# Segment sums of a Mamba-2 (SSD) branch: one fp32 matmul with fp32 operands, or two float32r matmuls over the high and low part of dt*A

## The chip, the cores and the metric

The kernel runs on one core of a Trainium2 chip. The time is device microseconds of one execution of the whole program, as the median of several runs. The profile is one execution taken by the hardware profiler. The engines of the core run their own instruction streams in order and wait for each other through semaphores: TensorE (PE, matmuls; PEld is its weight load), VectorE (DVE), ScalarE (ACT), GpSimd (POOL) and SyncE (SP, here only the queue of the weight transfers).

## The reference

The program is a two-layer decoder trunk on 256 tokens of width 1024. Layer 0 is SwiGLU, a mixer "AB", SwiGLU and a gated embedding; layer 1 has another mixer. The change lies in mixer AB, which runs two branches on the same input and joins them in one output projection:

```python
def ssd_chunked(x, dt, a, bmat, cmat):            # 16 heads, 4 groups, chunks of 128 tokens
    a_cum = cumsum(dt * a)                        # per head, within a chunk
    seg = a_cum[:, :, :, None] - a_cum[:, :, None, :]
    decay = exp(where(causal, seg, -inf))
    scores = einsum('bclgn,bcsgn->bclsg', cc, bc)
    y_diag = einsum(..., scores[..., None] * decay, xdt)
    ...                                           # plus the state carried from chunk 0 to chunk 1
def s5_mixer(u, ...):                             # second branch
    ...                                           # complex linear recurrence, giving y
    y = gelu(y)
    return y * sigmoid(y @ w_glu + b_glu)
def mixer_ab(x, ...):
    return concatenate([ssd_mixer(...), s5_mixer(...)], -1) @ w_out
```

## The kernel before, in words

Every large fp32 product is made of three float32r matmuls: each operand is split into a high part (rounded by ScalarE: names with `h`, as `wh`, `yh`, `xh`) and the rest (by VectorE: `wl`, `yl`, `xl`). Weights arrive in units of 1 MB (`wst`) and are split when they arrive.

The order of the instructions on each engine is set when the program is built: a scheduler places them, within the data dependencies and the buffers that a tile's tag has (`bufs=2`: the third tile of a tag waits until the first has been read). A tag's buffers go round in the order in which the code asks for tiles.

Mixer AB (`mixer_ab`) has, in the part that matters here:

- **S5 branch.** Eight batches give `s5y`; ScalarE copies each into `G`. When the second half of `G` is complete, ScalarE applies Gelu to it, GpSimd's queue writes it to DRAM (`ydram`) and reads it back transposed (`yT`), ScalarE and VectorE split it (`yh`, `yl`), and TensorE uses it in the 192 matmuls of `s5_outputs` (`glu`: eight channel tiles of 24). Half of the 24 need only the first half of `G`. After each channel tile come `th` (tanh, ScalarE), `gt` (VectorE), and its split `s5h`, `s5l`.
- **SSD branch.** For each of four groups `ssd_decays` makes a score tile `sc` (masked: `scm`) and for each of two chunks the product `R` = lower-triangular mask times dt*A (VectorE, 128x512), the segment sums `seg` = `strict` x `R` (TensorE), `E` = exp(seg) (ScalarE) and `E`*`scm` (VectorE). `ssd_heads` multiplies (`yp`, `cp`), adds and gates (`y`), takes the squares (`sq`, ScalarE) for a norm and scales; `finish_heads` transposes (`yT_ssd`) and splits (`xh_ssd`, `xl_ssd`). The decays of group 0 are emitted earlier, in `ab_inputs` (`first`).
- **Join.** `out_project` (`acc_ab`) multiplies the S5 parts and then the SSD parts with the output weights.

PSUM tiles `sc`, `seg`, `cp`, `ea_ps` and the S5 tiles share the tag `mm` with two buffers; `yp` and `yT_ssd` share `tr` with two. `sq` has two buffers of its own, and so has `gt`.

Gelu and Exp are in different function tables of ScalarE; a change of table is an instruction of its own (ACT_TABLE_LOAD).

Of the kernel before, what the change touches and what calls it, by code (L numbers as in the profile page):

```python
# [17 lines left out]
P = 128  # L18
D = 1024
NTOK = 256  # L20
NT = 2
# [12 lines left out]
def f32(ap):  # L34
    return ap.bitcast(F32)
# [298 lines left out]
def bc(ap, axis, n):  # L334

    shape = list(ap.shape)
    shape.insert(axis, n)
    return ap.unsqueeze(axis).broadcast_to(shape)
# [390 lines left out]
def s5_outputs(g, pool, yT, yh, yl):  # L729

    nc = g.nc
    hb = pool.tile([P, KT], F32, tag="hb", name="hb", bufs=1)
    nc.scalar.mul(hb, g.cols("bglu"), 0.5)
    sh = pool.tile([P, KT, NTOK], F32R, tag="sh", name="s5h", bufs=1)
    sl = pool.tile([P, KT, NTOK], F32R, tag="sl", name="s5l", bufs=1)
    for u in range(4):
        pieces = g.w.unit()
        for j in range(2):
            ct = 2 * u + j
            wh, wl = (p.rearrange("p (k c) -> p k c", k=KT) for p in pieces[j])  # L740
            ps = g.ps.tile([P, NTOK], F32, tag="acc", name=f"glu_{ct}", bufs=4)
            for k in range(KT):
                nc.tensor.matmul(ps, wh[:, k, :], yh[:, k, :], start=k == 0, stop=False)
                nc.tensor.matmul(ps, wh[:, k, :], yl[:, k, :], start=False, stop=False)
                nc.tensor.matmul(ps, wl[:, k, :], yh[:, k, :], start=False, stop=k == KT - 1)
            th = pool.tile([P, NTOK], F32, tag="th", name=f"th_{ct}", bufs=2)
            nc.scalar.activation(th, ps, AF.Tanh, scale=0.5, bias=hb[:, ct:ct + 1])
            gt = pool.tile([P, NTOK], F32, tag="gt", name=f"gt_{ct}", bufs=2)
            by_token = lambda ap: ap.rearrange("p (s c) -> p c s", s=4)
            nc.vector.scalar_tensor_tensor(gt.rearrange("p (c s) -> p c s", s=4), by_token(th[:, :]), 1.0,  # L750
                                           by_token(yT[ct // 4][:, ct % 4, :]), op0=ALU.add, op1=ALU.mult)
            nc.scalar.mul(sh[:, ct, :], gt, 0.5)
            nc.vector.scalar_tensor_tensor(sl[:, ct, :], gt, 0.5, f32(sh[:, ct, :]), op0=ALU.mult, op1=ALU.subtract)
    return sh, sl


def ssd_steps(g, pool, raw):

    nc = g.nc
    ps = g.ps.tile([P, NT, 16], F32, tag="mm", name="dt_ps", bufs=2)  # L760
    for t in range(NT):
        nc.tensor.matmul(ps[:, t, :], raw[:, t * P:(t + 1) * P], g.cst("fold")[0:32, :], start=True, stop=True)
    row = pool.tile([P, 48], F32, tag="abrow", name="abrow", bufs=1)
    nc.scalar.dma_start(row, g.abrow.broadcast_to([P, 48]))
    v = pool.tile([P, NT, 16], F32, tag="dtv", name="dtv", bufs=1)
    nc.vector.tensor_tensor(v, ps, bc(row[:, 0:16], 1, NT), op=ALU.add)
    e = softplus_terms(g, v, [P, NT, 16], pool, "dt")
    nc.vector.tensor_scalar(v, v, 0.0, None, op0=ALU.max)
    dt = pool.tile([P, NT, 16], F32, tag="dt", name="dt", bufs=1)
    nc.vector.scalar_tensor_tensor(dt, e, 2.0, v, op0=ALU.mult, op1=ALU.add)  # L770
    A = pool.tile([P, 16], F32, tag="A", name="A", bufs=1)
    nc.scalar.activation(A, row[:, 16:32], AF.Exp)
    dtA = pool.tile([P, NT, 16], F32, tag="dtA", name="dtA", bufs=1)
    nc.vector.scalar_tensor_tensor(dtA, dt, -1.0, bc(A[:, :], 1, NT), op0=ALU.mult, op1=ALU.mult)
    return dt, dtA, row[:, 32:48]


def ssd_carry(g, pool, dtA):
# [22 lines left out]
def ssd_decays(g, pools, gi, steps, Bt, Ct):  # L801
# [1 line left out]

    nc = g.nc
    pool, pr, pe, bufs = pools
    dtA = steps[1]
    hs = slice(4 * gi, 4 * gi + 4)
    sc = g.ps.tile([P, 384], F32, tag="mm", name=f"sc_{gi}", bufs=2)
    nc.tensor.matmul(sc[:, 0:256], Bt[:, gi, 0:P], Ct[:, gi, :], start=True, stop=True)
# [2 lines left out]
    nc.vector.tensor_tensor(scm, sc, g.cst("mask3"), op=ALU.mult)  # L812
    Ms = []
    for t in range(NT):
        R = pr(f"R_{gi}_{t}").rearrange("p (h c) -> p h c", h=4)
        nc.vector.tensor_tensor(R, bc(g.cst("incl"), 1, 4), bc(dtA[:, t, hs], 2, P), op=ALU.mult)
        sp = g.ps.tile([P, 4, P], F32, tag="mm", name=f"seg_{gi}_{t}", bufs=2)
        nc.tensor.matmul(sp, g.cst("strict"), R, start=True, stop=True)
        E = pe(f"E_{gi}_{t}").rearrange("p (h c) -> p h c", h=4)
        nc.scalar.activation(E, sp, AF.Exp)  # L820
        if t == 0:
            end = g.small.tile([P, 4], F32, tag="end", name=f"end_{gi}")
            nc.scalar.copy(end, E[:, :, P - 1])
        nc.vector.tensor_tensor(E, E, bc(scm[:, 256 * t:256 * t + P], 1, 4), op=ALU.mult)
        Ms.append(E)
# [101 lines left out]
def mixer_ab(g, ln):  # L927
    with g.tc.tile_pool(name="ab", bufs=2) as pool:
# [4 lines left out]
        with g.tc.tile_pool(name="abssd", bufs=2) as ssd:  # L933
            st = new_xT(g, "ssd")
            dec, ys = {}, {}
            ev = lambda name: pool.tile([P, 512], F32, tag="ev", name=name, bufs=2)
            ea = ssd_carry(g, ssd, steps[1])
            for gi in range(6):
                if gi < 4:
# [17 lines left out]
def ab_inputs(g, pool, s5pool, yh, yl):  # L957
# [41 lines left out]
    def recur(b):  # L999
# [3 lines left out]
        if b == 3:  # L1003
# [15 lines left out]
    xs_in(1)  # L1019
    recur(6)  # L1020
    recur(7)
    first = ssd_decays(g, (pool, lambda n: pool.tile([P, 512], F32, tag="ev", name=n, bufs=2),
                           lambda n: pool.tile([P, 512], F32, tag="xsT", name=n, bufs=2), 1), 0, steps, *BC)
    z_in(1)
    return BC, xs, szs, steps, yT, half[-1], first
# [492 lines left out]
```

## Time and profile before

| | us |
|---|---|
| median of three runs (1236.95 to 1238.12) | 1237.29 |
| profiled execution, its own time | 1236.71 |
| span of that execution, first to last instruction | 1234.9 |
| TensorE busy | 1202.8 (97%) |
| VectorE busy | 848.5 (69%) |
| ScalarE busy | 621.1 (50%) |

1.8 us of the profiled execution lie around its span. The granted TensorE clock was 0.996 of full speed over the span. Most of the time goes to the feed-forward blocks; mixer AB's part that the change touches lies between 360 and 450 us of the span.

### The profile page before, as it was taken

The page shows a single profiled execution, that of the slowest core. Times are in us where ns is not written, and L with a number is a line of the kernel's source. Part 1 is how long each engine was busy: PE and PEld are TensorE (multiplying, and loading weights), DVE is VectorE, ACT ScalarE, POOL GpSimd, SP SyncE. Part 2 cuts the span into 40 slices and gives each one's busy share as a digit, 9 for nine tenths or more (in the row PEclk, how much of TensorE's full clock was granted, in tenths as well). Part 3 has the DMA queues.
Part 4 walks back from the last instruction along what each step waited for, and adds up shares of the span by engine and source line. Part 5 has one row for each costly group of instructions (what it writes and reads, how often), then busy time and mean ns, then how long its engine had stood idle before and what let it go on. Part 6 is the DMA issues. An engine that isn't in the chain of part 4 may idle for free.

```text
span 1234.9 us, 16234 instructions
## 1 busy us (share of the span) xinstructions
PE 1202.8 (97%) x6274; PEld 1011.3 (82%) x6274; DVE 848.5 (69%) x1353; ACT 621.1 (50%) x944; POOL 48.5 (4%) x78
## 2 busy tenths in 40 slices
PE   6999999899999999999999999999999899999998
PEld 4888788699997878888887888887888778888886
DVE  6998874779879876555567554546689776545466
ACT  6566765444535635444536444443575535444434
POOL 0000000020101000000000000000100010000000
PEclk9999999999999999999999999999999999999999
DMA  7676778687842647555535655554633227555532
GB/s 267 218 253 241 248 259 320 219 289 263 278 140 72 222 143 254 177 198 180 195 137 204 217 192 186 189 190 165 227 122 137 103 80 255 185 193 182 197 144 102
DMA packets 40797, 242.12 MB, mean 196 GB/s; under 512 B 4848, under 2 KB 5520, under 8 KB 17040
## 3 DMA queue, kind: packets, MB, share of 16 engines
q1 hardware_dynamic: 30672, 206.06, 48.2%
q0 software_dynamic: 3952, 18.88, 4.3%
q10 hardware_dynamic: 6096, 16.16, 3.9%
q8 instruction: 49, 0.80, 0.3%
q14 instruction: 28, 0.23, 0.1%
HBM read 224.30 MB, written 16.78 MB: 195 GB/s over the span
## 4 chain that ended last, share of the span: by engine, by line
PE 72%; issue 5%; DVE 3%; DMA 1%; POOL 0%; ACT 0%; DVEq 0%; ACTq 0%; POOLq 0%
PE gu_f L72 10%; PE gu_f L71 10%; PE gu_f L70 9%; PE acc_f L72 5%; PE acc_f L70 5%; PE acc_f L71 5%; PE acc_ple L71 1%; PE acc_ab L70 1%; PE acc_ab L72 1%; PE acc_ab L71 1%; PE acc_ple L72 1%; PE acc_ple L70 1%; PE ht_f L209 1%; PE lv_h L1140 1%; PE lv_g L1140 1%
## 5 line engine op out<-in xcount | busy, mean ns | idle before, releaser
L62 DVE TENSOR_TENSOR wl<-wst,wh 128x1024 fp32r<-128x1024 f32 (+1 forms) x378 | 453.6, 1216 | 269.2 <-ACT wh L61 262.7
L61 ACT CAST wh<-wst 128x1024 fp32r<-128x1024 f32 (+1 forms) x378 | 386.7, 1045 | 319.8 <-PE gu_f L72 108.0
L70 PE MATMUL acc_f<-wh,hh_f 128*128 128x512 f32 x352 | 137.4, 391 | 1.2 <-ACT hh_f L212 1.2
L71 PE MATMUL acc_f<-wl,hh_f 128*128 128x512 f32 x352 | 137.7, 391 | 0.0
L72 PE MATMUL acc_f<-wh,hl_f 128*128 128x512 f32 x352 | 136.3, 392 | 0.2 <-DVE hl_f L213 0.2
L70 PEld LDWEIGHTS acc_f<-wh,hh_f 128*128 128x128 f32 x352 | 66.1, 188 | 15.4 <-ACT hh_f L212 2.1
L72 PEld LDWEIGHTS acc_f<-wh,hl_f 128*128 128x128 f32 x352 | 66.1, 188 | 14.1 <-DVE hl_f L213 0.7
L71 PEld LDWEIGHTS acc_f<-wl,hh_f 128*128 128x128 f32 x352 | 66.1, 188 | 13.5
L70 PE MATMUL gu_f<-wh,xh_in 128*128 128x512 f32 x176 | 70.9, 408 | 5.9 <-ACT wh L61 5.9
L205 ACT ACTIVATE sg_f<-gu_f 128x256 f32<-128x256 f32 x88 | 33.7, 384 | 75.1 <-PE gu_f L72 73.3
L70 PE MATMUL gu_f<-wh,xh_ple 128*128 128x512 f32 x176 | 69.7, 396 | 1.6 <-ACT xh_ple L112 1.6
L71 PE MATMUL gu_f<-wl,xh_in 128*128 128x512 f32 x176 | 70.7, 403 | 0.0
L70 PE MATMUL gu_f<-wh,xh_cd 128*128 128x512 f32 x176 | 69.8, 396 | 0.5 <-ACT xh_cd L112 0.5
L70 PE MATMUL gu_f<-wh,xh_ab 128*128 128x512 f32 x176 | 69.7, 396 | 0.5 <-ACT xh_ab L112 0.5
L72 PE MATMUL gu_f<-wh,xl_in 128*128 128x512 f32 x176 | 70.1, 399 | 0.0
L72 PE MATMUL gu_f<-wh,xl_ab 128*128 128x512 f32 x176 | 69.0, 392 | 0.7 <-DVE xl_ab L113 0.7
L72 PE MATMUL gu_f<-wh,xl_cd 128*128 128x512 f32 x176 | 69.0, 392 | 0.7 <-DVE xl_cd L113 0.7
L71 PE MATMUL gu_f<-wl,xh_cd 128*128 128x512 f32 x176 | 68.8, 391 | 0.2 <-DVE wl L62 0.2
L71 PE MATMUL gu_f<-wl,xh_ab 128*128 128x512 f32 x176 | 68.8, 391 | 0.2 <-DVE wl L62 0.2
L72 PE MATMUL gu_f<-wh,xl_ple 128*128 128x512 f32 x176 | 68.7, 392 | 0.0
L71 PE MATMUL gu_f<-wl,xh_ple 128*128 128x512 f32 x176 | 68.6, 390 | 0.0
L206 DVE TENSOR_TENSOR sg_f<-sg_f,gu_f 128x256 f32<-128x256 f32 x88 | 36.5, 416 | 27.2 <-ACT sg_f L205 27.2
(470 smaller groups left out, 2397.0 us busy)
## 6 DMA issues: line engine op xcount, KB each, us to landing
wst<-in_wall_dram SPq DMA_DIRECT2D x185, 1024.0 KB, 4.9
s5d<-s5pk POOLq DMA_DIRECT2D x8, 896.0 KB, 4.7
s5d<-s5pe POOLq DMA_DIRECT2D x8, 768.0 KB, 3.8
row<-in_lnr_dram SPq DMA_DIRECT2D x12, 512.0 KB, 6.4
W<-s5d ACTq DMA_DIRECT2D x8, 512.0 KB, 6.5
Q<-s5d ACTq DMA_DIRECT2D x8, 512.0 KB, 5.5
tab<-s5d ACTq DMA_DIRECT2D x8, 384.0 KB, 3.8
wst<-in_wall_dram SPq DMA_DIRECT2D x4, 512.0 KB, 6.4
```

Of the source, the lines that this page charges most:

```text
L61: ops = [nc.scalar.copy(wh[:, c], src[:, c])]
L62: ops.append(nc.vector.tensor_tensor(wl[:, c], src[:, c], f32(wh[:, c]), op=ALU.subtract))
L70: nc.tensor.matmul(out, xh, wh, start=first, stop=False)
L71: nc.tensor.matmul(out, xh, wl, start=False, stop=False)
L72: nc.tensor.matmul(out, xl, wh, start=False, stop=last)
L205: nc.scalar.activation(sg, ps[t][:, 0:256], AF.Silu)
L206: nc.vector.tensor_tensor(sg, sg, ps[t][:, 256:512], op=ALU.mult)
L209: nc.tensor.transpose(tp[:, k, :], sg[:, k * P:(k + 1) * P], g.ident)
L1140: nc.tensor.matmul(lp[0:m, n * t + j], xt[:, 0:m], xt.rearrange("p (a s b) -> p a s b", s=2, b=b)[:, :, 1, :], start=True, stop=True)
```

## The change

`dtA` is split once into a float32r part `dtAh` (ScalarE) and the rest `dtAl` (VectorE), and `strict`, a matrix of zeros and ones, is copied once to float32r. `R` is made of `dtAh` on VectorE as before. A second tile `Rl` is made of `dtAl` on ScalarE, head by head: four instructions of 128x128 for each of eight tiles. `seg` is the sum of two float32r matmuls. To make room for `Rl`, `gt` loses its two buffers and takes those of `sq`. For group 0, `R` and `Rl` share the two buffers that `R` had.

```diff
@@ s5_outputs
-            gt = pool.tile([P, NTOK], F32, tag="gt", name=f"gt_{ct}", bufs=2)
+            gt = pool.tile([P, NTOK], F32, tag="sq", name=f"gt_{ct}", bufs=2)
@@ ssd_steps
-    return dt, dtA, row[:, 32:48]
+    sh = pool.tile([P, NT, 16], F32R, tag="dtAh", name="dtAh", bufs=1)
+    sl = pool.tile([P, NT, 16], F32, tag="dtAl", name="dtAl", bufs=1)
+    nc.scalar.copy(sh, dtA)
+    nc.vector.tensor_tensor(sl, dtA, f32(sh), op=ALU.subtract)
+    strict = pool.tile([P, P], F32R, tag="strict", name="strict_r", bufs=1)
+    nc.scalar.copy(strict, g.cst("strict"))
+    return dt, dtA, row[:, 32:48], (f32(sh), sl, strict)
@@ ssd_decays
-    dtA = steps[1]
+    dh, dl, strict = steps[3]
...
-        R = pr(f"R_{gi}_{t}").rearrange("p (h c) -> p h c", h=4)
-        nc.vector.tensor_tensor(R, bc(g.cst("incl"), 1, 4), bc(dtA[:, t, hs], 2, P), op=ALU.mult)
+        R = pr(f"R_{gi}_{t}", F32R).rearrange("p (h c) -> p h c", h=4)
+        Rl = pr(f"Rl_{gi}_{t}", F32R).rearrange("p (h c) -> p h c", h=4)
+        nc.vector.tensor_tensor(R, bc(g.cst("incl"), 1, 4), bc(dh[:, t, hs], 2, P), op=ALU.mult)
+        for h in range(4):
+            nc.scalar.mul(Rl[:, h], g.cst("incl"), dl[:, t, hs.start + h:hs.start + h + 1])
         sp = g.ps.tile([P, 4, P], F32, tag="mm", name=f"seg_{gi}_{t}", bufs=2)
-        nc.tensor.matmul(sp, g.cst("strict"), R, start=True, stop=True)
+        nc.tensor.matmul(sp, strict, R, start=True, stop=False)
+        nc.tensor.matmul(sp, strict, Rl, start=False, stop=True)
@@ mixer_ab
-            ev = lambda name: pool.tile([P, 512], F32, tag="ev", name=name, bufs=2)
+            ev = lambda name, dt: (ssd if name[1] == "l" else pool).tile([P, 512], dt, tag="ev", name=name, bufs=2)
```

The order of the three engines around it changes at these places (a tile's last number tells its buffer's birth, and differs between the two programs).

First, ScalarE between the last copy into `G` and the first Exp after the Gelu of `G`'s second half. Before (`E_0_3537` and `E_1_3546` are the two chunks of group 0, `E_0_3659` is group 1):

```order
L707 COPY G_3109<-s5y_3514 128x256
L733 ACTIVATE hb<-lc 128x8
L820 ACT_TABLE_LOAD
L820 ACTIVATE E_0_3537<-seg_0_3535 128x512
L823 COPY end_3539<-E_0_3537 128x4
L820 ACTIVATE E_1_3546<-seg_1_3544 128x512
L784 ACTIVATE ea<-ea_ps 128x16
L713 ACT_TABLE_LOAD
L713 ACTIVATE G_3109<-G_3109 128x1024
L820 ACT_TABLE_LOAD
L820 ACTIVATE E_0_3659<-seg_0_3657 128x512
```

And in the changed kernel, from the instruction behind the copy on (`Rl_0_3674` and `Rl_1_3689` belong to group 1, `Rl_1_3555` to group 0, chunk 1; `E_1_3564` is group 0, chunk 1):

```order
L825 ACTIVATE Rl_0_3674<-cs,dtAl 128x128 x4
L825 ACTIVATE Rl_1_3689<-cs,dtAl 128x128 x4
L830 ACT_TABLE_LOAD
L830 ACTIVATE E_0_3549<-seg_0_3546 128x512
L825 ACTIVATE Rl_1_3555<-cs,dtAl 128x128 x4
L733 ACTIVATE hb<-lc 128x8
L833 COPY end_3551<-E_0_3549 128x4
L790 ACTIVATE ea<-ea_ps 128x16
L713 ACT_TABLE_LOAD
L713 ACTIVATE G_3115<-G_3115 128x1024
L830 ACT_TABLE_LOAD
L830 ACTIVATE E_1_3564<-seg_1_3561 128x512
```

Twelve `Rl` instructions now stand ahead of the Gelu, and the second Exp of group 0 has moved from ahead of it to behind it.

Second, VectorE around the first `gt`. Before (`gt_3960` and `gt_3991` are channel tiles 0 and 1, `y_0_3824` and `y_1_3830` are group 2):

```order
L859 TENSOR_TENSOR cr_3867<-cp_3865,ea 128x256
L750 SCALAR_TENSOR_TENSOR gt_3960<-th_3958,yT_2948 128x256
L79 TENSOR_SCALAR rs_w_ssd_3764<-ss_3750 128x2
L865 TENSOR_TENSOR y_0_3824<-xs_2202,abrow 128x256
L865 TENSOR_TENSOR y_1_3830<-xs_2203,abrow 128x256
L62 TENSOR_TENSOR wl_1_4146<-wst_4139,wh_1_4145 128x1024
L750 SCALAR_TENSOR_TENSOR gt_3991<-th_3989,yT_2948 128x256
```

Now (`gt_4014` is channel tile 0; `y_0_3924` and `y_1_3930` are group 3, the last):

```order
L62 TENSOR_TENSOR wl_1_4310<-wst_4303,wh_1_4309 128x1024
L902 SCALAR_TENSOR_TENSOR xl_ssd<-yT_ssd_3897,lc,xh_ssd 128x128
L887 TENSOR_SCALAR y_0_3878<-y_0_3878,rs_r_ssd_3893 128x256
L887 TENSOR_SCALAR y_1_3884<-y_1_3884,rs_r_ssd_3893 128x256
L902 SCALAR_TENSOR_TENSOR xl_ssd<-yT_ssd_3812,lc,xh_ssd 128x128
L877 TENSOR_TENSOR y_1_3930<-y_1_3930,cr_3921 128x256
L902 SCALAR_TENSOR_TENSOR xl_ssd<-yT_ssd_3897,lc,xh_ssd 128x128 x3
L878 TENSOR_TENSOR y_0_3924<-y_0_3924,yp_3910 128x256
L878 TENSOR_TENSOR y_1_3930<-y_1_3930,yp_3910 128x256
L881 TENSOR_TENSOR y_0_3924<-y_0_3924,sz_0_3637 128x256
L881 TENSOR_TENSOR y_1_3930<-y_1_3930,sz_1_3639 128x256
L750 SCALAR_TENSOR_TENSOR gt_4014<-th_4012,yT_2954 128x256
```

The first `gt` has moved from ahead of the work of group 2 to behind the gating of group 3.

Third, TensorE of the changed kernel between channel tile 5 of the `glu` product (`glu_4162`) and channel tile 6 (`glu_4203`): the transposes of group 1 (`yT_ssd_3897`), the `yp` of group 3, and the transposes of group 2 (`yT_ssd_3943`).

```order
L745 MATMUL glu_4162<-yh,wl_1_4128 128x256
L613 MATMUL yT_ssd_3897<-cs,y_0_3793 128x128
L613 MATMUL yT_ssd_3897<-cs,y_1_3799 128x128
L613 MATMUL yT_ssd_3897<-cs,y_0_3793 128x128
L613 MATMUL yT_ssd_3897<-cs,y_1_3799 128x128
L865 MATMUL yp_3910<-xd_0_3858,E_0_3840 128x64 x4
L865 MATMUL yp_3910<-xd_1_3862,E_1_3855 128x64 x4
L613 MATMUL yT_ssd_3943<-cs,y_0_3878 128x128
L613 MATMUL yT_ssd_3943<-cs,y_1_3884 128x128
L613 MATMUL yT_ssd_3943<-cs,y_0_3878 128x128
L613 MATMUL yT_ssd_3943<-cs,y_1_3884 128x128
L743 MATMUL glu_4203<-yh,wh_0_4195 128x256
```

Before, channel tiles 6 and 7 followed tile 5 with only the transposes of group 1 between them, and the `yp` of group 3 and the transposes of groups 2 and 3 stood later, each between matmuls of `acc_ab`. Behind `acc_ab` the order is the same in both programs on every engine.

## Rows read from the trace of the kernel before

**Rows 1.** Page, part 1: busy time and share of the span.

```profile
PE 1202.8 (97%) x6274; PEld 1011.3 (82%) x6274; DVE 848.5 (69%) x1353; ACT 621.1 (50%) x944; POOL 48.5 (4%) x78
```

**Rows 2.** Busy time by stretch: length, PE, PEld, DVE, ACT, POOL, clock, DMA.

```profile
376.00:384.20 8.20, 6.47 (x32) 4.21 (x31) 8.20 (x20) 2.99 (x8) 2.90 (x4) 1.00 0.30 90
384.20:392.20 8.00, 7.99 (x50) 6.55 (x51) 7.21 (x17) 4.66 (x13) 1.36 (x1) 1.00 0.00 0
392.20:407.50 15.30, 15.30 (x130) 15.25 (x129) 15.29 (x34) 11.17 (x26) 1.60 (x2) 1.00 0.58 179
```

**Rows 3.** Chain of waits, 290 to 450 us: start, duration, what.

```profile
374.06 4.09 DMA ydram<-G
...
380.37 3.07 DMA yT<-ydram
383.54 0.63 ACT yh L724
384.21 0.74 PE glu L743 x4
384.95 2.07 PE seg L818 x4
...
389.60 0.23 PE glu L744 x2
...
407.93 0.24 PE acc_ab L70
...
412.83 1.73 PE yp L855 x16
...
417.88 0.44 PE yT_ssd L613 x4
```

**Rows 4.** Timeline of ScalarE, 366 to 374 us: start, duration, [idle before].

```profile
367.29 0.37 ACT L707 COPY G<-s5y 128x256 f32<-128x256 f32 x1 [7.02 <-PE s5y L705]
...
370.72 0.60 ACT L820 ACTIVATE E<-seg 128x512 f32<-128x512 f32 x1 [0.71 <-PE seg L818]
...
371.41 1.28 ACT L713 ACT_TABLE_LOAD   x1
372.70 1.06 ACT L713 ACTIVATE G<-G 128x1024 f32<-128x1024 f32 x1
```

**Rows 5.** Timeline of TensorE around one segment sum.

```profile
369.67 1.02 PE L818 MATMUL seg<-R,cs 128*128 128x512 f32 x2
370.52 0.29 PE L782 MATMUL ea_ps<-dtA,cs 128*128 128x16 f32 x2
```

**Rows 6.** Timeline of ScalarE: multiplications by a per-partition factor, two and one.

```profile
406.93 0.64 ACT L891 ACTIVATE xh_ssd<-yT_ssd,lc 128x128 fp32r<-128x128 f32 x2
...
412.53 0.37 ACT L891 ACTIVATE xh_ssd<-yT_ssd,lc 128x128 fp32r<-128x128 f32 x1 [1.81 <-DVE xl_ssd L892]
```

**Rows 7.** Timeline of VectorE, 380 to 399 us.

```profile
380.55 0.68 DVE L816 TENSOR_TENSOR R<-cs,dtA 128x512 f32<-128x512 f32 x1
381.15 0.74 DVE L868 TENSOR_TENSOR y<-y,yp 128x256 f32<-128x256 f32 x2
...
396.05 0.62 DVE L877 TENSOR_SCALAR y<-y,rs_r_ssd 128x256 f32<-128x256 f32 x2
...
396.90 1.23 DVE L62 TENSOR_TENSOR wl<-wst,wh 128x1024 fp32r<-128x1024 f32 x1
398.04 0.35 DVE L892 SCALAR_TENSOR_TENSOR xl_ssd<-yT_ssd,lc,xh_ssd 128x128 fp32r<-128x128 f32 x1
```

**Rows 8.** Timelines: first `gt` on VectorE, first `sq` of group 3 on ScalarE.

```profile
392.78 0.60 DVE L750 SCALAR_TENSOR_TENSOR gt<-th,yT 128x256 f32<-128x256 f32 x1
...
415.72 0.42 ACT L873 ACTIVATE sq<-y 128x256 f32<-128x256 f32 x1 [1.74 <-DVE y L871]
```

**Rows 9.** TensorE after its idle time in mixer CD, and the stretches behind it.

```profile
983.26 1.87 PE L1172 MATMUL o_g<-tok_gv,at_g 128*128 128x128 f32 x8 [3.37 <-DVE y_h L1189]
...
985.00:987.00 2.00, 2.00 (x12) 2.00 (x11) 1.43 (x4) 1.18 (x2) 0.17 (x1) 0.52 0.03 8
987.00:989.00 2.00, 2.00 (x18) 1.93 (x17) 1.42 (x3) 0.69 (x2) 0.83 (x1) 1.00 0.00 0
```

More of the change, by code (lines that the diff above doesn't have):

```diff
@@ L1021, in ab_inputs @@
     recur(7)
-    first = ssd_decays(g, (pool, lambda n: pool.tile([P, 512], F32, tag="ev", name=n, bufs=2),
+    first = ssd_decays(g, (pool, lambda n, dt: pool.tile([P, 512], dt, tag="ev", name=n, bufs=2),
                            lambda n: pool.tile([P, 512], F32, tag="xsT", name=n, bufs=2), 1), 0, steps, *BC)
```

## The prediction

> **What bounds the kernel now.** The page's busy times come first: TensorE works 97% of the span, the other engines far less [rows 1]. So a microsecond taken from TensorE's work is a microsecond of the program where TensorE has work waiting, and nothing where it stands for another engine. Which of the two holds is read by stretch. From 376 to 384.2 us TensorE is busy 6.47 of 8.20 us while VectorE is busy for all 8.20; from 384.2 to 407.5 TensorE has next to no idle time [rows 2]. The chain of waits tells what ends the first stretch: the Gelu of `G`'s second half is followed by its write to DRAM (4.09 us), the transposed read (3.07), the split `yh` (0.63), and at 384.21 the first `glu` matmul that needs it [rows 3]. Behind the split stands `yl`, which is VectorE's. So two engines set the end of the stretch: ScalarE by when the Gelu starts (372.70 [rows 4]), and VectorE by when it comes to `yl`. From there on TensorE is the bound, as long as the S5 outputs and the SSD heads are done beside it.
>
> **The segment sums.** Two fp32 sums stand at 369.67 and the next instruction begins at 370.52 [rows 5]: 0.85 us for two halves, which is one whole sum of 512 columns (the profile shows each fp32 matmul as two). A float32r matmul on 256 columns costs 0.12 (`glu` x2 0.23, x4 0.74 with its start [rows 3]), so 512 columns are 0.23 and the two passes 0.46. That is 0.39 saved for each sum, 3.1 us for eight. But all eight sums stand before the last wait of the stretch in which TensorE idles: six ahead of the wait for `yh`, the last two (2.07 us, x4 [rows 3]) behind it, yet ahead of the product with `yl`. What is saved there makes the wait longer, unless the wait itself ends sooner. I count it at nothing.
>
> **Step A: the Gelu is late.** `Rl` costs ScalarE four multiplications by a per-partition factor each. Two such on 128x128 take 0.64 and one 0.37 [rows 6], so each further one takes 0.27; I take 0.27, with 0.37 as the upper bound (no overlap) and nothing saved below it. The order puts twelve ahead of the Gelu: 3.24 us. The second Exp of group 0 (0.60, of which 0.50 is the step) with the wait ahead of it (0.71) moves behind the Gelu [rows 4]. Net: +2.0 us, Gelu at 374.7.
>
> A rule speaks to this. VectorE does `R`, 128x512, in one step of 0.60 (380.55 to 381.15 [rows 7]); ScalarE needs 4 x 0.27 = 1.08 for the same shape. The Trainium skill, "ScalarE: Activation LUTs", section "Rules for kernel authors", says that a plain multiplication belongs on VectorE and not on ScalarE; the trace agrees on the price. It does not on the place: VectorE is full in this stretch [rows 2], so that seven `Rl` there would delay `yl` by 4.2 us, against 2.0 for the Gelu.
>
> **Step B: `yl` is later still.** The Exp of group 0, chunk 1, now stands behind the Gelu (1.06) and one table load (1.28) [rows 4]: 374.7 + 1.06 + 1.28 = 377.05, done at 377.65. Group 1's segment sum needs its PSUM buffer (tag `mm` has two), and VectorE, in order, stands at its product with `scm`. From there to the first `yl` the order has 25 VectorE instructions: nine on 512 columns (five `E`, four `R`) by 0.60, two `scm` by 0.5, fourteen on 256 columns by 0.33 (`y` x2 is 0.74, a step of 0.33) [rows 7]: 5.4 + 1.0 + 4.6 = 11.0 us. That gives `yl` at 388.7. The last `scm` before it also releases the last segment sum, behind which the second `glu` matmul waits. Before, it came behind the two sums that begin at 384.95 [rows 3], by 0.85 for each [rows 5] at 386.6 (the four `seg` end at 387.0 as modelled). Now: 388.7 and one sum of 0.46, 389.2. **+2.6 us.** (The sixteen further `Rl` put `yh` at some 386, so it is not the last.) What of this is not work of TensorE is idle. Bound below: if VectorE finds its inputs as early as before, only step A counts, +2.0. Bound above: twelve instructions by 0.10 more, +1.2.
>
> **Step C: `gt` waits for the last group's `sq`.** The buffers of a tag go round. `gt` now comes behind the two `sq` of group 3, so it can't be written until these are read, and so not before `yp` of group 3, its gating and squares. Before, the first `gt` was at 392.78, and that `sq` at 415.72 [rows 8]: 23 us apart, with all of `glu` and a part of `acc_ab` between them as cover. The dependence turns this round: no `gt`, no free `th` (two buffers), so no third `th`, and no free PSUM buffer for `glu` tile 6 (tag `acc`, four buffers, tiles 2 to 5). TensorE comes to the end of tile 5, and `yp` of group 3 with two groups' transposes stand alone between it and tile 6. Let T be the end of tile 5:
>
> - A weight unit's split stands on both engines right there, and can't start before tile 5 has read its buffer: `wh` on ScalarE, 128x1024 as the Gelu, 1.06 [rows 4]; `wl` on VectorE 1.14 (396.90 to 398.04 [rows 7]). T+2.2.
> - VectorE then does one `xl_ssd` (0.35), two scalings (0.26 each) and one more `xl_ssd` (0.35) [rows 7], 1.2 us; only this last one, group 0's, frees the PSUM buffer (tag `tr`) that `yp` takes. `yp` starts at T+3.45, and before it TensorE has 0.45 of transposes [rows 3]: **3.0 us idle**.
> - `yp` takes 1.73 [rows 3], to T+5.2. The transposes of group 2 wait for the last `xl_ssd` of group 1: `xh_ssd` and `xl_ssd` take turns (ScalarE waits for VectorE's in [rows 6]), 0.37 + 0.35 for each of three quarters, to T+5.65.
> - VectorE adds `yp` twice and gates, three steps of 0.33 [rows 7], T+6.65. ScalarE then has the first `sq` (0.42 [rows 8]), an `xh_ssd` (0.37), the second `sq` (0.42), `s5h` (as a 128x256 copy, 0.37 [rows 4]) and the third `th` (as large, 0.42): T+8.65. The first `gt` (0.60 [rows 8]) fits between the first `sq` and `s5h`. `glu` tile 6 starts.
>
> Of the 8.65 us 0.45 + 1.73 + 0.45 = 2.63 is work that TensorE had to do anyway [rows 3]. **+6.0 us**: 3.0 ahead of `yp`, 0.45 behind it, 2.55 ahead of tile 6. Bounds: if the weight's split came beside tile 5, 2.2 less; if every hand-over costs 0.1 on top, 1 more.
>
> **Nothing behind it gives this back.** From 384.95 to 417.88 the chain runs over TensorE alone [rows 3], and behind `acc_ab` the order is the same; there is no wait left to shorten. `acc_ab` begins at 407.93 now [rows 3] and then at about 407.9 + 8.6 + 1.7 + 0.45 = 418.7, with the last group's SSD work ahead of it and no more inside it. The rest of the change (`dtAh`, `dtAl`, two copies, group 0's first chunk) lies near 303 us beside a full TensorE; should its few 0.3 us steps not be hidden, they are under 1 us.
>
> **The sum.** 2.6 + 6.0 = 8.6 us, less nothing. The profiled execution's 1236.71 becomes 1245.3; the median of the runs, 1237.29, is 0.58 above that execution, so **1245.9**.
>
> **Rivals.**
> - *The clock falls.* In mixer CD TensorE idled 3.37 us ahead of 983.26; from 985 to 987 it was granted 0.52 of its speed, 1.2 GHz for 2.4, and 1.00 again from 987 [rows 9]. The 3.0 us of step C is nearly as long. From 983.26 to 987 at that speed some 1.8 us are lost: 1247.7. Against it: the 0.45 of transposes splits what lies around, and this gap is the shorter. The Trainium skill, "TensorE: Matmul & The Clock Gate", section "Why this matters for your kernels", tells to leave no long idle gaps between bursts of matmuls, since the engine then falls back to half speed; by that rule this rival is the forecast. The trace agrees with it for 3.37 us [rows 9].
> - *Step C is covered:* other `glu` or `acc_ab` work fills in, or the waits are half as long. For it: before, `gt` and `yp` hid everywhere. Against it: TensorE takes its instructions in order, and the order has none there. Then only steps A and B count: 1239.9.
> - *Faster.* TensorE is the bound, and 3.1 us of its work goes: 1237.3 - 3.1 = 1234.2. It decides if the Gelu starts no later than 372.7 and `gt` waits for nothing. For it speaks the 97% [rows 1]; against it the 1.73 us (8.20 less 6.47) that TensorE idles already [rows 2], and twelve multiplications ahead of the Gelu.
> - *No change:* the saving and the delays cancel, 1237. It needs step C to be free and A to be hidden.
> - *Worse:* the fall of the clock with the upper bounds, over 1250.
>
> **How the numbers follow.** Chances: forecast 0.55 (its own range 1243.5 to 1248, from the bounds of B and C), clock 0.20, step C covered 0.13, faster 0.04, no change 0.05, worse 0.03. The range takes the first three and leaves out the last: 1239.5 to 1250, with about 0.85 inside. A measurement of this kernel tells 0.2%, 2.5 us, from no change; step C covered lies just there, at +2.6, and some of it counts as the same. Faster 0.05, same 0.08, slower 0.87.
>
> **What would show it.** Step A: Gelu at about 374.7. Step B: `yl` at about 388.7, with VectorE waiting near 377. Step C: TensorE idle some 3 us ahead of the last `yp` and some 2.4 ahead of `glu` tile 6, and the first `gt` right behind the first `sq` of group 3. Segment sums: 0.46 for a pair. Wrong it would be if `glu` tile 6 followed tile 5 with the transposes alone, if the Gelu kept its time, or if TensorE's idle time were made up before `acc_ab` ends.

## The result and the profile after

The changed kernel takes 1251.67 us (median of six runs, 1250.7 to 1255.49); the kernel before, run beside it, 1237.12. The ratio is 1.0117, with a 95% interval of 1.0103 to 1.0131: 14.5 us slower, where 8.6 were forecast, and above the stated range. The profiled execution has a span of 1249.0 us against 1234.9, and a mean granted clock of 0.989 against 0.996.

The page of the changed kernel, part 1 (busy time and share of the span), answers to [rows 1]:

```profile
PE 1208.8 (97%) x6274; PEld 1018.9 (82%) x6274; DVE 849.4 (68%) x1354; ACT 630.3 (50%) x978; POOL 48.6 (4%) x78
```

TensorE is busy for 6.0 us more, although eight fp32 sums were replaced by shorter ones: the same matmuls took longer. The windows of [rows 2] and three around the end of `glu` tile 5 (length, PE, PEld, DVE, ACT, POOL, clock, DMA share, GB/s):

```profile
376.00:384.20 8.20, 6.02 (x31) 4.69 (x31) 6.27 (x14) 7.15 (x18) 3.48 (x5) 0.91 0.42 124
384.20:392.20 8.00, 7.04 (x45) 5.75 (x44) 8.00 (x20) 6.04 (x19) 0.51 (x1) 1.00 0.02 7
392.20:407.50 15.30, 12.81 (x108) 12.52 (x106) 14.74 (x33) 9.49 (x20) 2.59 (x3) 1.00 0.49 153
404.00:409.00 5.00, 1.97 (x14) 1.73 (x14) 4.58 (x12) 2.81 (x8) 1.00 (x1) 0.92 0.78 242
409.00:414.00 5.00, 3.46 (x17) 3.06 (x16) 2.76 (x8) 1.53 (x6) 0.00 (x0) 0.50 0.74 304
414.00:419.00 5.00, 4.16 (x21) 4.17 (x22) 4.88 (x14) 3.96 (x12) 0.92 (x1) 0.56 0.00 0
```

There is TensorE idle time in every stretch that was full before, and the granted clock, 1.00 throughout in [rows 2], is 0.50 from 409 to 414 us: the lower of its two levels, 1.2 GHz.

ScalarE's timeline, with the rows that answer to [rows 4] (start, duration, what, [idle before]):

```profile
368.37 2.46 ACT L825 ACTIVATE Rl<-cs,dtAl 128x128 fp32r<-128x128 f32 x8
...
372.63 1.26 ACT L825 ACTIVATE Rl<-cs,dtAl 128x128 fp32r<-128x128 f32 x4
...
375.47 1.06 ACT L713 ACTIVATE G<-G 128x1024 f32<-128x1024 f32 x1
```

A further `Rl` costs 0.30 (2.46 for eight, less the 0.37 of one alone in [rows 6], by 7), not 0.27. The last copy into `G` ends 0.7 us later than in [rows 4], for reasons outside the change (below); counted from it the Gelu is 2.1 us late, where 2.0 were forecast. VectorE's first `yl` and first `gt`:

```profile
389.50 1.29 DVE L725 TENSOR_TENSOR yl<-yT,yh 128x512 fp32r<-128x512 f32 x2
...
413.37 0.60 DVE L750 SCALAR_TENSOR_TENSOR gt<-th,yT 128x256 f32<-128x256 f32 x1 [0.30 <-ACT sq L883]
```

`yl` stands 0.8 us behind its forecast of 388.7, 0.7 of it that same shift, and the first `gt` is indeed released by ScalarE's `sq`, where [rows 8] have it 23 us ahead of that. TensorE's timeline at the two places of the forecast:

```profile
372.79 0.40 PE L788 MATMUL ea_ps<-dtA,cs 128*128 128x16 f32 x2 [2.14 <-ACT E L830]
373.95 0.71 PE L828 MATMUL seg<-Rl,strict_r 128*128 128x512 f32 x1 [0.77 <-ACT Rl L825]
...
379.06 0.39 PE L827 MATMUL seg<-R,strict_r 128*128 128x512 f32 x1
379.29 0.39 PE L828 MATMUL seg<-Rl,strict_r 128*128 128x512 f32 x1
379.52 1.00 PE L865 MATMUL yp<-xd,E 128*128 128x64 f32 x8
...
404.42 0.60 PE L613 MATMUL yT_ssd<-cs,y 128*128 128x128 f32 x4
408.04 3.57 PE L865 MATMUL yp<-xd,E 128*128 128x64 f32 x16 [3.03 <-DVE xl_ssd L902]
411.40 1.06 PE L613 MATMUL yT_ssd<-cs,y 128*128 128x128 f32 x4
414.84 0.58 PE L743 MATMUL glu<-yh,wh 128*128 128x256 f32 x1 [2.37 <-ACT th L747]
```

A pair of sums takes 0.46 (379.06 to 379.52), as worked out. TensorE idles 3.03 us ahead of the last `yp` and 2.37 ahead of tile 6 (forecast 3.0 and 2.55), released by `xl_ssd` and by `th`, as forecast. The 0.45 us forecast behind `yp` is missing: the transposes follow it at once (411.40). And `yp` takes 3.36 us (408.04 to 411.40) where [rows 3] have 1.73. The same view in windows of 1 us (PE, clock, DMA share, GB/s) shows why:

```profile
374.00:375.00 1.00, 1.00 (x3) 0.53 0.00 0
...
377.00:378.00 1.00, 0.54 (x3) 0.76 0.06 25
378.00:379.00 1.00, 0.51 (x2) 1.00 1.01 418
...
408.00:409.00 1.00, 0.96 (x5) 0.60 0.89 242
...
418.00:419.00 1.00, 1.00 (x8) 0.78 0.00 0
```

Behind each group of gaps the clock falls, about where the waiting work begins: it is low from 374 to 377.5 and from 408.2 to 418.4.

Where the 14.1 us of the span come from, by the start of the same instruction in both traces:

| up to | before | after | added here | forecast |
|---|---|---|---|---|
| first `glu` matmul | 359.89 | 360.60 | 0.7 | 0 |
| last `cp` matmul (behind `yl`) | 390.98 | 394.99 | 3.3 | 2.6 |
| last `acc_ab` matmul | 453.66 | 466.65 | 9.0 | 6.0 |
| first `acc_cd` matmul in mixer CD | 988.47 | 1002.56 | 1.1 | 0 |

Each row compares two single executions. The first 0.7 us are not of the change: experiment 1, which has nothing changed there, shows the same 0.7, and over the sixteen traces (these two and one of each experiment) the first `glu` matmul lies anywhere from 359.3 to 362.7. Nor are the 1.1 us in mixer CD, where both programs have the same order; from the last `acc_ab` to the first `acc_cd` matmul the sixteen traces take 533.2 to 537.8 us. The idle time there is 3.37 us as in [rows 9], but the low clock behind it lasts longer:

```profile
995.00:997.00 2.00, 0.87 (x4) 0.57 0.95 397
...
1001.00:1003.00 2.00, 2.00 (x13) 0.72 0.00 0
```

In [rows 9] it was back at 1.00 by 987, 3.7 us after the work began again; here at some 1002.1, 6.0 us after (996.13).

### The profile page after: what moved, and what is told of

Its sections match the earlier page's. It is cut to its first block, busy times and chain, and to the rows that moved or that the text cites. A ratio compares the mean times of both kernels' runs of the same rounds, so it can differ in the third digit from the quotient of the medians.

```text
span 1249.0 us, 16266 instructions
## 1 busy us (share of the span) xinstructions
PE 1208.8 (97%) x6274; PEld 1018.9 (82%) x6274; DVE 849.4 (68%) x1354; ACT 630.3 (50%) x978; POOL 48.6 (4%) x78
## 4 chain that ended last, share of the span: by engine, by line
PE 89%; DVE 4%; ACT 3%; DMA 3%; issue 1%; ACTq 0%; POOL 0%; DVEq 0%; SPq 0%
PE gu_f L72 12%; PE gu_f L71 12%; PE gu_f L70 12%; PE acc_f L72 6%; PE acc_f L70 6%; PE acc_f L71 6%; DMA wst<-in_wall_dram 2%; PE ht_f L209 2%; DVE wl L62 1%; PE acc_ab L71 1%; PE acc_ab L70 1%; PE acc_ab L72 1%; PE s5v L682 1%; PE s5k L551 1%; PE s5y L705 1%
## 5 line engine op out<-in xcount | busy, mean ns | idle before, releaser
L72 PEld LDWEIGHTS acc_f<-wh,hl_f 128*128 128x128 f32 x352 | 66.1, 188 | 14.1 <-DVE hl_f L213 0.7
```

The lines of the kernel that those rows point to most:

```text
L72: nc.tensor.matmul(out, xl, wh, start=False, stop=last)
```

## The experiments

All but 3, 4 and 5 compute the whole reference. Each was timed beside the kernel before on the same chip. Because the executions of one kernel differ in how long the clock is low, a table of means stands at the end of this section.

**1 and 2. The buffer alone, and everything but the buffer.** The first edit is made to the kernel before, the second to the changed kernel:

```diff
-            gt = pool.tile([P, NTOK], F32, tag="gt", name=f"gt_{ct}", bufs=2)
+            gt = pool.tile([P, NTOK], F32, tag="sq", name=f"gt_{ct}", bufs=2)
```
```diff
-            gt = pool.tile([P, NTOK], F32, tag="sq", name=f"gt_{ct}", bufs=2)
+            gt = pool.tile([P, NTOK], F32, tag="gt", name=f"gt_{ct}", bufs=1)
```

> The kernel before with one line changed: gt takes the buffers of sq; segment sums stay fp32 with no low part. Theory (the buffer's round is most of the loss: about 5.5 us of TensorE idle around the last group's yp, and about 3.6 us more because the clock falls in it): 1243 to 1247 us, TensorE idle 2 to 3 us ahead of the last yp and again ahead of glu tile 6, granted clock at 0.5 behind the first gap. Rival 1 (the multiplications on ScalarE are the loss, the buffer is free): 1237 +-1, no idle there. Rival 2 (idle time alone, the clock doesn't fall here): 1242 to 1243.

> The changed kernel with gt in one buffer of its own instead of the two of sq. Theory: the loss at yp and glu tile 6 goes, the loss ahead of the product with yl stays (3.3 us in the changed kernel's trace, 1.5 of it the low clock from 374 to 378 us, behind an idle time of about 3 us): 1240 to 1241.5 us, Gelu at about 375.5, no TensorE idle above 0.5 us between 392 and 420 us. Rival 1 (ScalarE's extra work is the loss wherever gt lies): 1249 to 1252. Rival 2 (without the buffer's wait the saving of 3.1 us shows): 1234 to 1237.

Measured: the buffer alone 1249.12 us, ratio 1.009 (1.0073 to 1.0106); everything but the buffer 1241.17, ratio 1.0027 (1.0018 to 1.0036). So the one line about the buffer is 11 of the 14 us, and the rest of the change some 3. The first is 2 us above the range of its theory, with gaps and low clock at the places that it named; the second is within its theory's. TensorE's timeline with the buffer alone:

```profile
406.86 3.67 PE L855 MATMUL yp<-xd,E 128*128 128x64 f32 x16 [4.67 <-DVE xl_ssd L892]
...
413.76 0.58 PE L743 MATMUL glu<-yh,wh 128*128 128x256 f32 x1 [2.37 <-ACT th L747]
```

The gap ahead of `yp` is longer than in the changed kernel (4.67 for 3.03): TensorE reaches the end of tile 5 earlier, and ScalarE's split of the weights behind it also waits 1.64 us for their transfer. With `gt` in a buffer of its own TensorE has no idle time between 403 and 423 us.

**3 and 4. No low part, with either buffer.** The multiplications on ScalarE and the second pass are left out, so the decays have lower precision:

```diff
-        for h in range(4):
-            nc.scalar.mul(Rl[:, h], g.cst("incl"), dl[:, t, hs.start + h:hs.start + h + 1])
-        nc.tensor.matmul(sp, strict, R, start=True, stop=False)
-        nc.tensor.matmul(sp, strict, Rl, start=False, stop=True)
+        nc.tensor.matmul(sp, strict, R, start=True, stop=True)
```

> The changed kernel without the low part: no multiplications on ScalarE and one float32r matmul for each segment sum, so decays of lower precision; gt still takes the buffers of sq. Theory: the Gelu is back at about 373 and the loss ahead of yl is gone, the buffer's loss stays: 1243 to 1247, like the kernel before with the buffer alone. Rival 1 (ScalarE's work is the loss): 1235 to 1238. Rival 2 (TensorE is the bound, each sum saves 0.62 us, 5 us in all, which shows): 1238 to 1242.

> As the one before (one float32r matmul for each sum, no low part, lower precision), and gt in one buffer of its own. All costs of the change are gone and 5 us of TensorE work are saved. Theory (the sums stand ahead of waits that other engines and the DMA end): 1235.5 to 1237.5, with more TensorE idle between 370 and 385 us than the kernel before. Rival (TensorE's work is the bound): 1232 to 1233.

Measured: 1251.66, ratio 1.0121 (1.0102 to 1.0139), with the shared buffer, and 1240.49, ratio 1.0025 (1.0014 to 1.0036), with its own. Both fell outside every range that was given. Leaving out ScalarE's multiplications together with the second pass thus changes neither time. With the shared buffer this is not because they cost nothing: in the trace of 3 the last `cp` comes at 391.22 in place of 394.99, so the loss ahead of it is gone, but TensorE then idles 6.18 us ahead of the last `yp`, where the changed kernel has 3.03, and ScalarE waits 2.77 us there for a transfer of weights. The later wait takes what the earlier one gives back:

```profile
408.61 3.67 PE L861 MATMUL yp<-xd,E 128*128 128x64 f32 x16 [6.18 <-DVE xl_ssd L898]
```

With its own buffer, a kernel with 5 us less work on TensorE, the old order of the Gelu and no shared buffer is 2.5 us slower. TensorE's timeline of it:

```profile
371.07 1.00 PE L861 MATMUL yp<-xd,E 128*128 128x64 f32 x8
374.43 0.50 PE L824 MATMUL seg<-R,strict_r 128*128 128x512 f32 x1 [2.36 <-ACT E L826]
...
377.28 3.52 PE L861 MATMUL yp<-xd,E 128*128 128x64 f32 x16
...
408.36 0.50 PE L70 MATMUL acc_ab<-wh,s5h 128*128 128x512 f32 x1 [1.12 <-ACT th L747]
```

and its windows of 2 us:

```profile
376.00:378.00 2.00, 2.00 (x10) 0.54 0.30 70
...
384.00:386.00 2.00, 1.82 (x8) 0.50 0.00 0
386.00:388.00 2.00, 1.49 (x10) 0.90 0.00 0
```

With the short sum the second `seg` comes early, its `yp` fits in ahead, and TensorE then waits 2.36 us in one piece for the Exp behind Gelu and table loads. Behind that the clock is low from 376.2 to 386.4, and 16 `yp` matmuls take over 3.2 us, for 1.73 in [rows 3]. That made the theory of the clock, which the next runs tried. This trace gives it little of the loss, though: from the first to the last `glu` matmul this kernel takes 47.5 us and the kernel before 47.1, so what the low clock cost in that stretch, less what the shorter sums saved, is about 0.5. Another 1.12 us are idle ahead of the first `acc_ab`, at the end of a chain with a transfer of weights in it. Where the rest of the 2.5 us comes from stays open.

**5. The short sum four times.** To the kernel of experiment 4 (one pass, lower precision):

```diff
-            nc.tensor.matmul(sp, strict, R, start=True, stop=True)
+            for _ in range(4):
+                nc.tensor.matmul(sp, strict, R, start=True, stop=True)
```

> The kernel with one float32r matmul for each sum and gt in a buffer of its own, but each of the eight matmuls done four times over the same data (the last counts), so that TensorE is busy for as long as the fp32 sums kept it. New theory (what a shorter sum saves becomes idle time in a stretch that waits, the idle time comes together in one gap, and behind it the clock falls to half for up to ten us, which costs more than was saved): with 5.5 us of useless work added the time falls to that of the kernel before, 1237 to 1238.5 us, granted clock 1.00 from 366 to 390. Rival 1 (the loss of 2.5 us comes from the new order of the instructions, not from the clock): 1240 to 1241.5. Rival 2 (TensorE's work adds): 1243 or more.

Measured: 1239.51 (twelve runs, 1236.48 to 1243.15), ratio 1.0018 (1.0007 to 1.003). That lies between the theory's range and the first rival's. In the profiled execution the clock held (1.00 from 366 to 422), and from the first `glu` to the last `acc_ab` it is 0.7 us behind the kernel before, the kernel of experiment 4 1.9 (by the starts of the same instructions); most of the difference of 1.2 is the gap ahead of the first `acc_ab`, which this kernel hasn't. Five us of useless work cost nothing here, but the whole program is only 1 us faster than experiment 4, between two wide spreads. What made experiment 4 slower, the clock or the order, is not settled by it.

**6. Useless work ahead of the last `yp`,** in the changed kernel (`zr` is a matrix of zeros):

```diff
+            for k in range(24 if ct == 5 else 0):
+                nc.tensor.matmul(ps, zr, yh[:, k % KT, :], start=False, stop=k == 23)
```

> The changed kernel with 24 useless float32r matmuls (a zero matrix times yh, added to glu tile 5's sum, 2.9 us of TensorE) in the gap ahead of the last group's yp. Theory (part of the buffer's loss is the clock, which falls behind the 3.0 us of idle time): the work fits into the gap, yp takes 1.7 and not 3.4 us, and the time falls by 2 to 3.6 us against the changed kernel's 1251.7: 1248 to 1249.7; more stays lost if the second gap ahead of glu tile 6 lets the clock fall by itself. Rival (waits alone, the clock has no part): 1251.7 to 1253.

Measured: 1251.17, ratio 1.0109 (1.0094 to 1.0125): no faster, and between the two ranges. In its trace the stretch from the last `cp` to the last `acc_ab` adds 7.2 us in place of 9.0, and `yp` takes 2.0 us; but in this execution the clock was low from 372 to 392.8, where the changed kernel's was back at 377.5, and the last `cp` came 3.7 us later (398.67 for 394.99). Inconclusive.

**7. The Gelu early,** in the kernel before: its call moves ahead of group 0's decays.

```diff
     recur(7)
+    yT.append(s5_half_out(g, half[-1], 1, yh, yl))
     first = ssd_decays(g, ...
```

> The kernel before, with the Gelu of the second half of G and its transfers written ahead of group 0's decays, so that ScalarE does it ahead of both Exps; segment sums in fp32, gt as before. Theory (the stretch from 370 to 384 us is ended by the way of Gelu, DRAM write and transposed read, 1.7 us of TensorE idle there): Gelu at about 369 and yh some 3.5 us earlier; the Exps come 2.4 us later, so that TensorE idles more at 371 and less at 384: 1235 to 1237.5 if the clock holds. Rival 1 (the idle time at 371 grows over 2.3 us and the clock falls): 1239 to 1242. Rival 2 (VectorE ends the stretch, not the Gelu): 1237.5 to 1238.5.

Measured: 1236.02, ratio 0.9988 (0.9978 to 0.9998), as its theory had it. The Gelu starts at 368.97 in place of 372.70, and TensorE has `glu` work from 376 us on:

```profile
370.00:372.00 2.00, 0.48 (x3) 1.00 0.27 113
372.00:374.00 2.00, 1.67 (x6) 0.63 0.37 150
374.00:376.00 2.00, 2.00 (x6) 0.52 0.33 86
376.00:378.00 2.00, 2.00 (x18) 1.00 0.64 174
```

From 376 to 392 TensorE has no idle time, so the waits of [rows 2] are gone; a gap at 371 and some 3.4 us of low clock behind it give a part of the gain back.

**8. The low part on VectorE,** in the kernel of experiment 2:

```diff
-        for h in range(4):
-            nc.scalar.mul(Rl[:, h], g.cst("incl"), dl[:, t, hs.start + h:hs.start + h + 1])
+        nc.vector.tensor_tensor(Rl, bc(g.cst("incl"), 1, 4), bc(dl[:, t, hs], 2, P), op=ALU.mult)
```

> The changed kernel with the low part made by VectorE, in one instruction of 128x512 for each tile as the high part, and gt in one buffer of its own. It compares with the same kernel whose low part is made by ScalarE (1241.2). Theory of the prediction (VectorE is full in this stretch, so seven instructions of 0.60 there put yl 4 us later, against 2 us for the Gelu): 1242 to 1245. Rival (a plain multiplication costs less on VectorE, and the Gelu is early again): 1237.5 to 1240.5.

Measured: 1240.57, ratio 1.002 (1.0009 to 1.0031), beside 1241.17 with ScalarE: the same, below the range of the theory and just above its rival's. The working of the prediction for this case was wrong: the Gelu starts at 371.70, and the scheduler puts `yl` at 382.3, ahead of SSD work, which comes later instead.

**9 to 12. The early Gelu with useless work, with the whole change, and with both.** Experiment 9 does the fp32 sum of group 0, chunk 1 three times. Experiments 10 and 11 make the low part on VectorE, 12 on ScalarE behind the Gelu; all three have `gt` in its own buffer. Experiment 11 differs from 10 by this alone:

```diff
+        for _ in range(6 if (gi, t) == (0, 1) else 0):
+            nc.tensor.matmul(sp, strict, R, start=True, stop=True)
         nc.tensor.matmul(sp, strict, R, start=True, stop=False)
```

> The kernel with the early Gelu and fp32 sums, with the sum of group 0, chunk 1 done three times over the same data (1.7 us of useless TensorE work) in the idle time of 1.5 us at 370.5 us, behind which the clock fell from 372 to 376. Theory (the clock falls behind idle time and can be held by any work): clock 1.00 from 366 to 390 in the profile, 1234.5 to 1236 us where the early Gelu alone has 1236.0. Rival (the useless work only delays the Exp of that chunk and what follows): 1236.5 to 1238.

> All of the float32r change with the low part made by VectorE, gt in one buffer of its own, and the Gelu early. Theory (a shorter sum shows where TensorE has work waiting; with yh at about 378 the last sums stand among the glu matmuls): the early Gelu's 1236.0 less up to 2 us, 1234 to 1236, if the clock falls no longer than there. Rival 1 (the gap at 370 to 374 grows by what the sums save and the clock stays low for longer): 1237 to 1240. Rival 2 (nothing of the sums shows anywhere): 1236 to 1237.

> As the one before, with the high pass of group 0, chunk 1 done seven times over the same data (six useless matmuls, 1.4 us) to hold the clock in the gap. Theory: clock 1.00 or low for less than 2 us, 1233 to 1235.5, the fastest of all. Rival (the clock has no part in it): the same as the one before or 1 us more.

> All of the float32r change with the low part made by ScalarE as in the changed kernel, but for groups 1 to 3 behind the Gelu, gt in one buffer of its own, and the Gelu early. Theory (ScalarE has room once the Gelu is out): as the version with VectorE within 1 us, 1234 to 1236.5. Rival (twelve multiplications ahead of the Exps of group 1 keep TensorE waiting at 373 to 378, and the clock falls): 1238 to 1241.

Measured: 1238.62, ratio 0.9995 (0.9983 to 1.0007); 1242.67, ratio 1.0032 (1.0017 to 1.0047); 1236.85, ratio 0.9986 (0.9974 to 0.9999); 1245.34, ratio 1.0046 (1.003 to 1.0063). Experiment 9 held the clock in its profile (1.00 from 366 to 392), but its twelve runs lie between 1232.76 and 1240.45, and the median, just above both ranges, says nothing. Experiment 10 is slower than all its ranges, and 11 lies between its theory and its rival. By the medians six useless matmuls make the program 5.8 us faster from 10 to 11. TensorE's timeline and the window around it in 10:

```profile
371.95 0.40 PE L788 MATMUL ea_ps<-dtA,cs 128*128 128x16 f32 x2 [1.73 <-ACT E L829]
...
370.00:380.00 10.00, 8.00 (x42) 0.83 0.30 107
```

and in 11:

```profile
369.36 1.64 PE L827 MATMUL seg<-R,strict_r 128*128 128x512 f32 x6 [0.57 <-DVE R L823]
...
371.56 0.39 PE L788 MATMUL ea_ps<-dtA,cs 128*128 128x16 f32 x2 [0.33 <-ACT E L831]
...
370.00:380.00 10.00, 8.53 (x51) 1.00 0.31 107
```

The gap shrinks from 1.73 to 0.33 us, and the clock stays up. How much of the 5.8 us is that, the traces don't show: the two profiled executions took 1242.90 and 1241.68 us, the latter the slowest of its twelve, and it has a gap of 3.36 us ahead of the `glu` matmul at 402.13, with a low clock behind it. The scheduler also placed later `yp` and transposes otherwise. Experiment 12 went its rival's way, and 4 us beyond its range: the Exps of group 1 come late, and the clock is 0.50 from 376 to 388.

**13 and 14. Useless work in the gaps of the changed kernel.** Experiment 13 does the high pass of group 0, chunk 1 thirteen times in place of once; 14 adds the zero matmuls of experiment 6, and the transposes of group 2 four times.

> The changed kernel with the high pass of group 0, chunk 1 done thirteen times over the same data (twelve useless matmuls, 2.8 us) in the idle time of 2.1 us at 370 us; nothing else. Theory (of some 6 us that the clock costs, 1.5 to 3 come from this gap): clock 1.00 from 366 to 390 and 1248.5 to 1250.5, the fall behind the gap ahead of yp unchanged. Rival (the clock has no part, or the useless work delays the chain): 1251.5 to 1254.

> As the one before, and the 24 zero matmuls ahead of the last group's yp, and the transposes of group 2 done four times (1.3 us) ahead of glu tile 6: some 7 us of useless TensorE work in all. Theory: the clock stays at 1.00 from 366 to 425, yp takes 1.7 to 2.0 us, and the time is what the prediction gave for the waits alone, 1245 to 1247.5. Rival: 1251 to 1256, as the changed kernel or slower by the work.

Measured: 1252.78, ratio 1.0124 (1.0111 to 1.0138), and 1250.62, ratio 1.0109 (1.0092 to 1.0126; five runs, 1248.71 to 1254.38). Both theories missed; 13 lies in its rival's range, 14 just below its own. The clock holds through the filled gap, but the useless work also delays the Exp behind it, and TensorE idles at the next place. In 14:

```profile
380.66 0.51 PE L833 MATMUL seg<-R,strict_r 128*128 128x512 f32 x1 [2.52 <-ACT E L836]
...
412.51 2.00 PE L871 MATMUL yp<-xd,E 128*128 128x64 f32 x16 [1.41 <-DVE xl_ssd L909]
415.44 3.36 PE L613 MATMUL yT_ssd<-cs,y 128*128 128x128 f32 x16 [0.94 <-DVE y L884]
```

The last `yp` runs at full clock here, but 2.52 us of idle time have moved to 378, with a low clock from 382 to 385. In 13 the gap ahead of the last `yp` grew from 3.03 to 4.72 us.

**All executions by their mean clock.** Each execution has a time and a mean granted clock. Over all 213 for which both are on record, 0.001 of clock less goes with 0.76 us more within the executions of one kernel (one slope fitted to the deviations from each kernel's own means). The last column moves each kernel's mean to a clock of 0.994 by that slope:

| kernel | runs | mean us | mean clock | at 0.994 |
|---|---|---|---|---|
| before | 86 | 1238.1 | 0.9936 | 1237.8 |
| changed | 6 | 1252.6 | 0.9853 | 1246.0 |
| 1 buffer alone | 5 | 1248.7 | 0.9900 | 1245.6 |
| 2 own buffer | 11 | 1241.0 | 0.9908 | 1238.6 |
| 3 one pass, shared buffer | 5 | 1252.4 | 0.9842 | 1245.0 |
| 4 one pass, own buffer | 12 | 1240.8 | 0.9908 | 1238.4 |
| 5 as 4, four times | 12 | 1239.5 | 0.9929 | 1238.7 |
| 6 useless work ahead of `yp` | 4 | 1251.1 | 0.9880 | 1246.6 |
| 7 early Gelu | 12 | 1236.4 | 0.9938 | 1236.2 |
| 8 low part on VectorE | 12 | 1240.1 | 0.9920 | 1238.6 |
| 9 as 7, useless work | 12 | 1237.9 | 0.9926 | 1236.9 |
| 10 early Gelu, VectorE | 9 | 1242.6 | 0.9907 | 1240.0 |
| 11 as 10, useless work | 12 | 1237.1 | 0.9942 | 1237.2 |
| 12 early Gelu, ScalarE | 6 | 1244.3 | 0.9880 | 1239.8 |
| 13 useless work, first gap | 4 | 1253.0 | 0.9875 | 1248.1 |
| 14 useless work, all gaps | 5 | 1251.2 | 0.9906 | 1248.6 |

At an equal clock the changed kernel stands 8.2 us above the kernel before; the other 6.3 of the means' difference of 14.5 go with the clock. The last column is an estimate: one slope stands for every place where the clock can be low, also for those where TensorE only waits, and the changed kernel's own executions reach only from 0.981 to 0.989. It is a comparison of means, not an edit: no run held the clock in the changed kernel without moving its waits. Experiment 14, with the higher clock, stands 2.6 us above the changed kernel in this column; it paid for the clock with waits.

## Why the prediction was wrong

**The sum held the clock at full speed; that is the step that failed.** The fall of the clock stood beside the sum as a rival, with a chance of 0.20 and a price of 1.8 us; in the sum it counted for nothing. It happened, and cost more: in the trace 1.6 us in `yp` (3.36 for 1.73 [rows 3]) and about 1.6 in tile 6, whose first 16 matmuls stand 0.21 apart in place of 0.12. They account for what step C ran over its forecast: it took 9.0 us, and 5.8 without these 3.2, for 6.0. The two traces are 14.1 us apart, 5.5 more than the 8.6 of the sum: 3.0 are in step C, 1.1 in the fall in mixer CD, 0.7 in step B, and 0.7 were there ahead of the first `glu`. The price was taken from one fall, that of [rows 9], whose length isn't fixed: the same place took 1.1 us more in the changed kernel's trace. And it was looked for at one gap only: the low clock lasted over the next gap into tile 6. These are durations in one trace and not the effect of an edit; in experiments 6 and 14, where useless work let `yp` run in 2.0 us, other waits took the gain, and the program was about 1 us faster at most.

The total of the waits was near: 8.6 us forecast, 9.1 in the trace (3.3 and 5.8), 8.2 at an equal clock. The parts are less sure. At an equal clock the kernel with its own buffer stands only 0.8 us above the kernel before, and the shared buffer adds 7.4, where the forecast had 2.6 and 6.0. No run settles which is right, so the match of the total at an equal clock may be luck in part.

Point by point:

- *Segment sums:* 0.46 for a pair, as worked out. That the saved time turns to idle time was foreseen, and no run shows a gain from it. Experiment 4, the shorter sum without the low part, is 2.5 us slower by its median, and 0.6 above the kernel before at an equal clock; in its trace the saving became one longer gap with a low clock behind it, and by the last `glu` matmul it is 0.5 us behind. So "I count it at nothing" was not far off, and the rest of that loss has no cause shown.
- *Step A:* right, 2.1 us for 2.0. But experiments 3 and 4, which leave it out, are as slow as their counterparts with it (1251.66 and 1251.67; 1240.49 and 1241.17). In the trace of 3 a longer wait behind it, with a transfer of weights in it, took its place.
- *Step B:* the mechanism held. The chain of waits of the changed kernel runs over the late Exp and then over VectorE to the last `scm`:

```profile
377.84 0.61 ACT E L830
...
379.50 1.20 DVE R L823 x2
...
389.12 0.48 DVE scm L818
389.64 0.50 PE seg L827
...
405.81 1.14 DVE wl L62
...
407.73 0.27 DVE xl_ssd L902
408.04 3.58 PE yp L865 x16
```

  The Exp came at 377.84 and `yl` at 389.50, both as forecast but for the 0.7 us of shift. Behind the last `scm` stood not one sum but a sum and a `cp`, and the `glu` matmul with `yl` came at 390.61 where it had come at 386.49: without the 0.7 of shift 3.4 us later, for 2.6. The low clock from 374 to 377.5 cost nothing here: the chain runs over ScalarE at that time.
- *Step C:* its links are those of the chain above, down to `wl` and `xl_ssd` ahead of `yp`; idle 3.0 and 2.4 us as forecast, without the 0.45 between them, and 9.0 us in all for 6.0 by the clock. Experiments 1 and 2 show that the shared buffer is its cause. (`acc_ab` begins at 407.07 in the kernel before; the 407.93 that the prediction reads from [rows 3] is a later matmul of it. In the changed kernel it begins at 422.69, not at 418.7. No term of the sum uses this.)
- *The rule on VectorE and ScalarE:* weighed and set aside because VectorE is full. The Trainium skill, "ScalarE: Activation LUTs", section "Rules for kernel authors", would have the low part on VectorE; experiment 8 did so and came out the same, so neither the rule nor the argument against it decided here.
- *The clock rival's page* (the Trainium skill, "TensorE: Matmul & The Clock Gate", section "Why this matters for your kernels", no long idle gaps between bursts): by that rule this rival was the forecast. The trace agrees for 3.03 us here. It is less regular than the rule: the clock fell behind 2.36 us in experiment 4 too, and didn't behind 3.37 us in three traces (last section); there the measurement decides.

Two versions have an interval that lies below the kernel before, both barely: the early Gelu alone, 1236.02 (ratio 0.9988, 0.9978 to 0.9998), and with it the whole float32r change, own buffer, low part on VectorE and the useless work, 1236.85 (0.9986, 0.9974 to 0.9999).

## What to carry to other kernels

When a tile is given the buffers of another tag, look for what stands before it in the round: the wait is for those readers, wherever the scheduler has put them. A shorter TensorE instruction in a stretch that waits for other engines lengthens a gap, and behind the gap the clock may fall; count idle time at more than its own length where TensorE has work of its own to do behind it (3.2 us here, in `yp` and tile 6), and not where it goes on waiting (nothing at 374 us). A delay that ends ahead of a second wait isn't simply added to it: experiment 3 removed the first and got a longer second. Where executions differ in the mean clock, compare kernels at an equal clock too before the rest is put down to waits.

## What was not expected of the hardware

The same idle time is followed by a low clock in one execution and not in another. The 3.37 us in mixer CD, between the same instructions in all sixteen traces, have a low clock about them in thirteen; in those of experiments 2, 3 and 8 it stays up, and the work up to the first `acc_cd` takes 3.6 us, for 5.2 in the kernel before and 6.4 in the changed one. Experiment 2:

```profile
988.02 1.16 PE L1182 MATMUL o_g<-tok_gv,at_g 128*128 128x128 f32 x8 [3.37 <-DVE y_h L1199]
...
988.00:990.00 2.00, 1.98 (x17) 1.98 (x18) 1.96 (x4) 0.78 (x2) 0.22 (x1) 1.00 0.48 201
```

An idle time of 1.9 us near 226 us, ahead of all that was changed, is followed by one in nine of the sixteen, the changed kernel (227.3 to 230.7) among them, and not in the kernel before.

The length varies as well: behind the 3.37 us it was back 3.7 us after the work began in one trace and 6.0 in the other; behind the gaps from 370 us on, it lasted 3.4 us in the changed kernel and some 20 in experiment 6. The kernel before alone spreads from 1234.4 to 1241.6 us over 86 runs, with mean clocks from 0.997 down to 0.991.
